# A third of the first token block's expert products moved to TensorE, and the softmax of the routing weights cut in two

## The chip, the cores and the metric

The kernel runs on one core of a Trainium2 chip. The metric is the device time of one execution in microseconds (us), taken as the median of several runs. The engines are TensorE (PE; its weight loads are shown as PEld), VectorE (DVE), ScalarE (ACT), GpSimd (POOL) and SyncE (SP). Each takes its own instructions in order and waits on semaphores for the others.

## The reference, cut to what matters

One block of a model: 256 tokens of 2048 values, a modulation, a mixer of two attention-like groups, and then a layer of 16384 single-neuron experts (PEER). Only the expert layer is touched. For each token, 8 heads choose 16 experts each:

```python
vs, pos = lax.top_k(cand, PEER_TOPK)          # 16 of the pairs of keys, for each token and head
idx = e1 * N_KEYS + e2                        # which expert
g = jax.nn.softmax(vs, axis=-1)               # routing weights over the 16
def block(args):                              # for a block of 128 tokens
    xb, ib, gb = args
    u = jnp.take(expert_down, ib, axis=0)     # 128 tokens x 8 heads x 16 rows of 2048 values
    a = jax.nn.gelu(jnp.einsum('td,thkd->thk', xb, u), approximate=False)
    w = (gb * a).astype(xb.dtype)
    vv = jnp.take(expert_up, ib, axis=0)
    return jnp.einsum('thk,thkd->td', w, vv)
```

## The kernel before, in words

The tokens lie on the 128 partitions in two blocks, t = 0 and t = 1. After the mixer, the hidden values `hf` (features on the partitions) are turned by TensorE into `ht[t]` (tokens on the partitions) by `by_tokens`. `head_scores(h)` computes a head's query and its scores against the keys, on TensorE. `head(t, h)` then finds the 16 chosen experts of a head for a block: `keys` (top 16 of each half, then of the candidate sums, in `vs` and `pos`) and `chosen` (the indices into `idx[t]`), all on DVE. It puts 16 rows on the list `ready`.

A "row" in what follows is one such item (t, k): 128 expert rows of 2048 float32, one for each token of the block, 1.05 MB in all. `issue` takes rows from `ready` and starts an indirect DMA from POOL for each (tile `rows`), as long as one of the buffers named in `homes` is free; a buffer tag has two buffers, so four tags make eight rows in flight. `dot` takes the oldest row in flight, and DVE multiplies it by `ht[t]` in place and adds it up into one column of `dots[t]`; then `issue` runs again, and the new DMA waits on POOL until that buffer has been read. There are 128 rows for a block, 256 in all. `ready` is kept sorted, so that all rows of t = 0 go ahead of those of t = 1.

The order of everything from here on is the program's order on each engine, kept by the wrapper `InOrder`. That wrapper is why nearly all these instructions carry line 69 in the profile; they are told apart by their tiles. The loop over `behind` runs the heads (0,1) to (0,7) and then (1,1) to (1,7), with `dot` between them: a head of t = 0 comes when at most two rows of t = 0 wait, one of t = 1 when at most eight rows of it wait and none of t = 0. After head (0,7) comes `softmax(0)`: DVE subtracts the largest score, ACT takes the exponential, DVE sums, inverts and scales, so that `ev[0][:, 2]` (tile `e`) holds the routing weights. `turned(0, [0, 1])` turns the expert numbers on TensorE. When the last row of t = 0 has been taken, `first_half` calls `turned(0, [2])` (ACT: Gelu of `dots[0]`; DVE: product with the weights; TensorE turns it) and emits `first_ones` and `gates` for the eight groups of 16 tokens of the first block. These build one-hot matrices on ACT (tiles `o`), multiply them on TensorE into a map of gate values, copy it out on ACT (`stage`, `kept`) and send it to device memory (`gd`). They run beside the rows of t = 1.

After head (1,7) the same is done for t = 1: `softmax(1)`, `turned(1, [0, 1])`, six `first_ones` on ACT, and the rows that are left. Then come `turned(1, [2])`, the gates of the second block, and a long last stage in which TensorE multiplies the gate map by the expert table `up` (a quarter of the columns is taken by gathered rows `upr` on DVE).

Of the kernel before, what the change touches and what calls it, by code (L numbers as in the profile page):

```python
# [7 lines left out]
F32 = mybir.dt.float32  # L8
# [4 lines left out]
AF = mybir.ActivationFunctionType  # L13
ALU = mybir.AluOpType
# [4 lines left out]
P = 128  # L19
D = 2048  # L20
KD = D // P
# [12 lines left out]
PEER_H = 8  # L34
# [46 lines left out]
def hybrid_block(ctx: ExitStack, tc: tile.TileContext, x, c, wada, cst, shp, wst, wg, wmv, wfv,  # L81
                 wmo, wout, wq, down, up, upr, out):
    nc = tc.nc
# [7 lines left out]
    def bank(shape, tag="ps"):  # L91
        return psum.tile(shape, F32, tag=tag, name=tag)
# [57 lines left out]
    ident = sh[:, 0:P]  # L150
# [79 lines left out]
    issue = [0]  # L230
# [109 lines left out]
    def gemm_p(src, rh, rl, w=None):  # L340

        wh, wl = w or weights(src, [P, KD, P])
        some_ada()
        o = bank([P, T])
        for k in range(KD):
            nc.tensor.matmul(o, wh[:, k], rh(k), start=(k == 0), stop=False)
            nc.tensor.matmul(o, wh[:, k], rl(k), start=False, stop=False)
            nc.tensor.matmul(o, wl[:, k], rh(k), start=False, stop=(k == KD - 1))
        return o
# [7 lines left out]
    def gemm_t(src, dst, ch):  # L357

        o = [bank([P, 512]) for _ in range(NT)]
        for kq in range(4):  # L360
# [9 lines left out]
            if kq == 3:  # L370
                for t in range(NT):
# [15 lines left out]
                                 op1=ALU.bypass)  # L387
# [208 lines left out]
    for b in range(KD):  # L596
        o = gemm_p(wout[b], lambda k: cath[k // 8][:, k % 8], lambda k: catl[k // 8][:, k % 8])
        g = mod[:, GATE1 * KD + b:GATE1 * KD + b + 1]
# [11 lines left out]
    hf = const.tile([P, KD, T], F32, tag="hs", name="hf")  # L610
# [36 lines left out]
    nc = AllInOrder(tc, nc)  # L647
# [12 lines left out]
    pg = ctx.enter_context(tc.tile_pool(name="pg", bufs=2))  # L660
    pk_cm = tc.tile_pool(name="pk", bufs=2)
    pk = pk_cm.__enter__()
# [64 lines left out]
    ev = [pb.tile([P, 3, PEER_H, TOPK], F32, name=f"e{t}", bufs=1) for t in range(NT)]  # L727
    idx = [pb.tile([P, HK], U32, name=f"idx{t}", bufs=1) for t in range(NT)]
    dots = [pg.tile([P, HK], F32, bufs=1, name=f"dots{t}") for t in range(NT)]

    def flat(tile, h0, h1):
        return tile[:, h0:h1].rearrange("p h k -> p (h k)")
# [31 lines left out]
    def issue():  # L764
        while ready:
            tag = homes[turn[0] % len(homes)]
            if sum(f[0] == tag for f in flight) == 2:
                return
            turn[0] += 1
            t, k = ready.pop(0)  # L770
            u = ring.tile([P, D], F32, tag=tag, name="rows", bufs=2)
            nc.gpsimd.indirect_dma_start(u, None, down, bass.IndirectOffsetOnAxis(ap=idx[t][:, k:k + 1], axis=0))
            flight.append((tag, t, k, u))

    def dot(n=1):

        for _ in range(n):
            if not flight:
                return
            _, t, k, u = flight.pop(0)  # L780
            nc.vector.scalar_tensor_tensor(u, u, 1.0, ht[t], op0=ALU.mult, op1=ALU.mult,
                                           accum_out=dots[t][:, k:k + 1])
            issue()

    def softmax(t):
        g = ev[t][:, 2]
        nc.vector.tensor_tensor(g, vs[t], vs[t][:, :, 0:1].to_broadcast([P, PEER_H, TOPK]), op=ALU.subtract)
        nc.scalar.activation(g, g, AF.Exp)
        gs = pk.tile([P, PEER_H], F32, tag="gs", name="gs")
        nc.vector.reduce_sum(gs, g, axis=AX.X)  # L790
        nc.vector.reciprocal(gs, gs)
        nc.vector.tensor_tensor(g, g, gs[:, :, None].to_broadcast([P, PEER_H, TOPK]), op=ALU.mult)

    def turned(t, parts):

        if 2 in parts:
            w = flat(ev[t][:, 2], 0, PEER_H)
            nc.scalar.activation(dots[t], dots[t], AF.Gelu)
            nc.vector.tensor_tensor(w, w, dots[t], op=ALU.mult)
        ep = bank([P, len(parts), P], "at")  # L800
        for i, p in enumerate(parts):
            nc.tensor.transpose(ep[:, i], flat(ev[t][:, p], 0, PEER_H), ident)
        nc.scalar.activation(est[t][:, parts[0]:parts[-1] + 1], ep, AF.Copy)
# [9 lines left out]
    def first_ones(tb, engine=None):  # L813

        half, t0 = divmod(tb * TB, P)
        if 2 * HB - 4 <= tb < 2 * HB - 2:
            o1 = px.tile([P, TB, P], F32, name="o1")
        else:
            o1 = (ring, pg)[tb % 2].tile([P, TB, P], F32, tag=("lo", "o1")[tb % 2], name="o1", bufs=2)
        if engine is None:  # L820
            for tl in range(TB):
                t = t0 + tl
                nc.scalar.activation(o1[:, tl], iota, AF.Abs, bias=est[half][:, 0, t:t + 1], scale=-1.0)
            nc.scalar.activation(o1, o1, AF.Relu, scale=-1.0, bias=one)
        else:
            engine.tensor_tensor(o1, iota[:, None, :].to_broadcast([P, TB, P]),
                                 est[half][:, 0, t0:t0 + TB, None].to_broadcast([P, TB, P]), op=ALU.is_equal)
        ones_at[tb] = o1

    def gates(tb):  # L830
        if not kept:
            kept.append(const.tile([P, GK, T, 8], F32, tag="hs", name="kept"))
        stage = pg.tile([P, 16 - GK, TB, 8], F32, tag=f"q{tb % 2 if tb >= HB else 0}", name="stage", bufs=1)
        ts = slice(tb * TB, (tb + 1) * TB)
        half, t0 = divmod(tb * TB, P)
        col = est[half]
        o1 = ones_at.pop(tb)
        for t8 in range(0, TB, 8):

            o2 = pg.tile([P, 8, P], F32, tag="o2", name="o2")  # L840
            for tl in range(8):
                t = t0 + t8 + tl
                if half:
                    nc.vector.tensor_scalar(o2[:, tl], iota, col[:, 1, t:t + 1], col[:, 2, t:t + 1],
                                            op0=ALU.is_equal, op1=ALU.mult)
                else:
                    nc.scalar.activation(o2[:, tl], iota, AF.Abs, bias=col[:, 1, t:t + 1], scale=-1.0)
            if not half:
                nc.scalar.activation(o2, o2, AF.Relu, scale=-1.0, bias=one)
                for tl in range(8):  # L850
                    t = t0 + t8 + tl
                    nc.scalar.activation(o2[:, tl], o2[:, tl], AF.Copy, scale=col[:, 2, t:t + 1])
                out_of_psum()
            for t4 in range(0, 8, 4):
                gp = bank([P, 4, P], "at")
                for i in range(4):
                    nc.tensor.matmul(gp[:, i], o1[:, t8 + t4 + i], o2[:, t4 + i], start=True, stop=True)
                full.append((gp, stage, tb, t8 + t4))
            if half:
                out_of_psum()  # L860
# [14 lines left out]
    def head_scores(h):  # L875
        qs = [query(2 * h)]
        qs.append(query(2 * h + 1))
        scores(2 * h, qs[0])
        if h == 0:
            for j in range(4):  # L880
                by_tokens(0, j)
        scores(2 * h + 1, qs[1])

    def head(t, h):
        keys(h, t, later[t][:, h])
        chosen(t, h, h + 1)
        issue()

    def waiting(t):
        return sum(r[0] == t for r in ready)  # L890
# [3 lines left out]
    def first_half():  # L894

        of_first = sum(f[1] == 0 for f in flight) + waiting(0)
        if halves[0] == 0 and of_first == 8:
            homes[:] = ["raw", "rawb", "hi"]
            halves[0] = 1
        if halves[0] == 1 and of_first == 0:  # L900
            halves[0] = 2
            turned(0, [2])
            for tb in range(4):
                first_ones(tb)
            for tb in range(HB):
                gates(tb)
                if tb + 4 < HB:
                    first_ones(tb + 4)
            out_of_psum()
# [11 lines left out]
    for i, (t, h) in enumerate(behind):  # L921
        while waiting(t) > (2, 8)[t] or (t and waiting(0)):
            dot()
            first_half()
        head(t, h)
        if i < 2:
            head_scores(4 + 2 * i)
            head_scores(5 + 2 * i)
        if i == 1:
            homes[:] = ["raw", "rawb", "hi", "lo"]  # L930
        if (t, h) == (0, PEER_H - 1):
            halves[0] = 0
            softmax(0)
            turned(0, [0, 1])
    softmax(1)
    turned(1, [0, 1])
    pk_cm.__exit__(None, None, None)
    px_cm = tc.tile_pool(name="px", bufs=2)
# [30 lines left out]
    while flight:  # L969
        dot()  # L970
        if len(ready) == 4:
            homes[:] = ["raw", "rawb"]
    turned(1, [2])
    steps = [(b, q) for b in range(P // 4) for q in range(KU // 4)]
    loaded = [load(up[b, q], [P, 4, 512]) for b, q in steps[:4]]
# [29 lines left out]
    o = [bank([P, 2, T], "ps" if i < 4 else "at") for i in range(KU // 2)]  # L1005
# [45 lines left out]
    for s, (b, q) in enumerate(steps):  # L1051
# [13 lines left out]
        if b % 3 == 0 and q == 0 and later_mods:  # L1065
            k = later_mods.pop(0)
# [4 lines left out]
        for i in range(4):  # L1071
            ob = o[2 * q + i // 2][:, i % 2]
            cols = slice(i * P, (i + 1) * P)
            for j in range(4):
# [5 lines left out]
                                 stop=(b == P // 4 - 1 and j == 3 and i % 2 == 1), **flags)  # L1080
# [93 lines left out]
```

## Time and profile before

| | |
|---|---|
| median of three runs | 1920.65 us (1917.27 to 1929.78) |
| the profiled execution's own time | 1930.43 us |
| its span, first to last instruction | 1928.7 us |
| DVE busy | 1678.6 us (87%) |
| PE busy | 1269.6 us (66%) |
| ACT busy | 813.8 us (42%) |
| POOL busy | 832.9 us (43%) |
| rows of t = 0 and t = 1, with their heads | about 545 to 1332 us of the span |

Times in rows are microseconds from the span's start, unless marked ns. "Granted clock" is TensorE's clock as a share of 2.4 GHz: 1.00 is the upper of its two levels, 0.50 the lower, 1.2 GHz. "DMA share" is the mean busy share of the core's 16 DMA engines; it can read a little over 1. A row in which an engine is said to wait names the last thing it waited for.

### The profile page before, as it was taken

The page shows a single profiled execution, that of the slowest core. Times are in us where ns is not written, and L with a number is a line of the kernel's source. Part 1 is how long each engine was busy: PE and PEld are TensorE (multiplying, and loading weights), DVE is VectorE, ACT ScalarE, POOL GpSimd, SP SyncE. Part 2 cuts the span into 40 slices and gives each one's busy share as a digit, 9 for nine tenths or more (in the row PEclk, how much of TensorE's full clock was granted, in tenths as well). Part 3 has the DMA queues.
Part 4 walks back from the last instruction along what each step waited for, and adds up shares of the span by engine and source line. Part 5 has one row for each costly group of instructions (what it writes and reads, how often), then busy time and mean ns, then how long its engine had stood idle before and what let it go on. Part 6 is the DMA issues. An engine that isn't in the chain of part 4 may idle for free. (4 is left out here: it accounts for less than half of the span.)

```text
span 1928.7 us, 24437 instructions
## 1 busy us (share of the span) xinstructions
PE 1269.6 (66%) x9078; PEld 1189.8 (62%) x9078; DVE 1678.6 (87%) x2383; ACT 813.8 (42%) x1324; POOL 832.9 (43%) x516
## 2 busy tenths in 40 slices
PE   5899999998999910000022111203699999999998
PEld 3899977798987810000022111103699999999998
DVE  7888898897788799999999999789788888988884
ACT  4332384585431000000195444491555555555552
POOL 0000000000003466776766677573267777677760
PEclk9999999999999965555556555556899999999999
DMA  9977767787869999999999999988699999999992
GB/s 395 370 314 291 283 257 302 289 326 282 326 252 398 421 376 405 378 385 365 422 369 394 389 366 382 363 322 338 229 368 349 352 377 378 374 369 391 369 349 100
DMA packets 126648, 663.70 MB, mean 344 GB/s; under 512 B 13377, under 2 KB 38337, under 8 KB 55745
## 3 DMA queue, kind: packets, MB, share of 16 engines
q1 hardware_dynamic: 69186, 326.58, 44.3%
q0 software_dynamic: 57344, 335.58, 43.4%
q8 instruction: 71, 1.16, 0.2%
q14 instruction: 47, 0.39, 0.0%
HBM read 647.42 MB, written 14.68 MB: 343 GB/s over the span
## 5 line engine op out<-in xcount | busy, mean ns | idle before, releaser
L69 POOL DMA_INDIRECT rows<-in_down,idx x256 | 477.6, 1866 | 843.2 <-DMA raw<-in_wq 579.6
L69 DVE SCALAR_TENSOR_TENSOR rows<-rows,ht 128x2048 f32<-128x2048 f32 x256 | 572.6, 2287 | 35.3 <-DMA rows<-in_down,idx 34.4
L69 POOL DMA_INDIRECT rows<-in_upr,idx x256 | 355.1, 1387 | 201.1 <-DVE acc L69 88.1
L69 PE MATMUL ps<-w,whi 128*128 128x256 f32 x2048 | 353.9, 278 | 9.3 <-ACT w L69 8.6
L69 PEld LDWEIGHTS ps<-w,whi 128*128 128x128 f32 x2048 | 310.8, 189 | 9.8 <-ACT w L69 8.8
L69 PE MATMUL ps<-w,wlo 128*128 128x256 f32 x1024 | 284.1, 277 | 0.0
L69 PE MATMUL at<-o,o 128*128 128x128 f32 x512 | 93.3, 361 | 249.4 <-ACT o L69 240.2
L69 PEld LDWEIGHTS at<-o,o 128*128 128x128 f32 x512 | 88.2, 266 | 254.6 <-ACT o L69 244.2
L69 PE MATMUL at<-sh,e 128*128 128x128 f32 x6 | 2.2, 433 | 347.3 <-DVE e L69 347.3
L69 PEld LDWEIGHTS at<-sh,e 128*128 128x128 f32 x6 | 1.1, 206 | 348.2 <-issue 348.2
L69 PEld LDWEIGHTS ps<-w,wlo 128*128 128x128 f32 x1024 | 193.4, 189 | 0.0
L69 DVE SCALAR_TENSOR_TENSOR acc<-rows,e,acc 128x512 f32<-128x512 f32 x254 | 189.2, 745 | 2.7 <-DMA rows<-in_upr,idx 1.1
L69 PE MATMUL at<-w,wht 128*128 128x256 f32 x1536 | 189.5, 283 | 0.0
L69 PEld LDWEIGHTS at<-w,wht 128*128 128x128 f32 x1536 | 186.4, 192 | 0.0
L69 ACT ACTIVATE whi<-raw 128x1024 fp32r<-128x1024 f32 x128 | 128.6, 1053 | 116.2 <-PE ps L69 67.8
L69 DVE TENSOR_TENSOR wlo<-raw,whi 128x1024 fp32r<-128x1024 f32 x128 | 155.5, 1218 | 23.7 <-ACT whi L69 22.1
L113 ACT ACTIVATE whi<-raw 128x2048 fp32r<-128x2048 f32 x65 | 124.1, 1911 | 117.3 <-PE at L315 24.9
L114 DVE TENSOR_TENSOR wlo<-raw,whi 128x2048 fp32r<-128x2048 f32 x65 | 148.4, 2285 | 24.5 <-ACT whi L113 24.3
L69 PE MATMUL ps<-hf,raw 128*128 128x256 f32 x512 | 116.4, 388 | 7.7 <-DMA raw<-in_wq 6.5
L69 ACT ACTIVATE wht<-raw 128x1024 fp32r<-128x1024 f32 x64 | 64.4, 1054 | 116.0 <-PE at L69 101.1
L69 PEld LDWEIGHTS ps<-hf,raw 128*128 128x128 f32 x512 | 98.4, 194 | 23.7 <-DMA raw<-in_wq 9.0
L69 ACT ACTIVATE o<-sh,est 128x128 f32<-128x128 f32 x352 | 105.9, 393 | 0.4 <-PE at L69 0.4
(248 smaller groups left out, 2750.3 us busy)
## 6 DMA issues: line engine op xcount, KB each, us to landing
raw<-in_up SPq DMA_DIRECT2D x96, 1024.0 KB
raw<-in_wada SPq DMA_DIRECT2D x45, 1024.0 KB
early<-in_wada SPq DMA_DIRECT2D x44, 1024.0 KB
raw<-in_wst SPq DMA_DIRECT2D x32, 1024.0 KB
raw<-in_wout SPq DMA_DIRECT2D x16, 1024.0 KB
raw<-in_wq SPq DMA_DIRECT2D x16, 1024.0 KB
gd<-stage SPq DMA_DIRECT2D x16, 768.0 KB
g<-gd SPq DMA_DIRECT2D x12, 1024.0 KB
```

Of the source, the lines that this page charges most:

```text
L69: return self.tc.keep_in_program_order(f(*args, **kwargs))
L113: nc.scalar.activation(hi, raw, AF.Copy)
L114: nc.vector.tensor_tensor(lo, raw, hi.bitcast(F32), op=ALU.subtract)
```

## The change: what it does

- From head (0,2) on (`by_pe[1]`), every third row of t = 0 by the running count goes to `pe_dot` in place of DVE's product. TensorE turns the row's sixteen 128x128 parts (four to a bank of tag "ps"), ACT copies each bank to a tile `ut` (tag "o1"), and `issue` starts the next gather, which waits on POOL until TensorE has read the row.
- `cross` multiplies the turned row by `hf` in 16 accumulating matmuls, so that a 128x128 product of all tokens' rows with all tokens' hidden values stands in a bank. It is emitted one `pe_dot` later, behind the next row's transposes.
- `diagonal` takes the diagonal of that product on DVE: one 128x128 multiplication by the identity with a sum, into the column of `dots[0]`. It is emitted two rows after `cross`. `all_crossed` does what is left when the last row of t = 0 has been taken, ahead of `turned(0, [2])`.
- `softmax(t)` is cut: `exps(t)` (subtraction and exponential) stays where `softmax(t)` was; the sum, inverse and scaling come later. For t = 0 that is directly ahead of `turned(0, [2])`, for t = 1 when four rows are left in `ready`. The small tile `gs` moves from pool `pk` to pool `pg`.

```diff
+    by_pe = [0, False]
+    turning = []
+    crossed = []
+
+    def pe_dot(k, u):
+        ut = pg.tile([P, KD, P], F32, tag="o1", name="ut")
+        for j in range(4):
+            tp = bank([P, 4, P], "ps")
+            for i in range(4):
+                nc.tensor.transpose(tp[:, i], u[:, (4 * j + i) * P:(4 * j + i + 1) * P], ident)
+            nc.scalar.activation(ut[:, 4 * j:4 * j + 4], tp, AF.Copy)
+        if crossed:
+            cross(*crossed.pop(0))
+        crossed.append((k, ut))
+
+    def cross(k, ut):
+        o = bank([P, P], "at")
+        for i in range(KD):
+            nc.tensor.matmul(o, ut[:, i], hf[:, i, 0:P], start=(i == 0), stop=(i == KD - 1))
+        turning.append((k, o, by_pe[0] + 2))
+
+    def diagonal(k, o):
+        d = pk.tile([P, P], F32, tag="tk", name="d")
+        nc.vector.scalar_tensor_tensor(d, o, 1.0, ident, op0=ALU.mult, op1=ALU.mult, accum_out=dots[0][:, k:k + 1])
+
+    def all_crossed():
+        while crossed:
+            cross(*crossed.pop(0))
+        while turning:
+            diagonal(*turning.pop(0)[:2])
+
     def dot(n=1):
         for _ in range(n):
             if not flight:
                 return
             _, t, k, u = flight.pop(0)
+            by_pe[0] += 1
+            if by_pe[1] and t == 0 and by_pe[0] % 3 == 0:
+                pe_dot(k, u)
+                issue()
+                continue
+            if turning and turning[0][2] <= by_pe[0]:
+                diagonal(*turning.pop(0)[:2])
             nc.vector.scalar_tensor_tensor(u, u, 1.0, ht[t], op0=ALU.mult, op1=ALU.mult,
                                            accum_out=dots[t][:, k:k + 1])
             issue()
 
-    def softmax(t):
+    def exps(t):
         g = ev[t][:, 2]
         nc.vector.tensor_tensor(g, vs[t], vs[t][:, :, 0:1].to_broadcast([P, PEER_H, TOPK]), op=ALU.subtract)
         nc.scalar.activation(g, g, AF.Exp)
-        gs = pk.tile([P, PEER_H], F32, tag="gs", name="gs")
+
+    def softmax(t):
+        g = ev[t][:, 2]
+        gs = pg.tile([P, PEER_H], F32, tag="gs", name="gs", bufs=1)
         nc.vector.reduce_sum(gs, g, axis=AX.X)
...
@@ first_half
             halves[0] = 2
+            all_crossed()
+            softmax(0)
             turned(0, [2])
...
@@ the loop over behind
         if i == 1:
             homes[:] = ["raw", "rawb", "hi", "lo"]
+            by_pe[1] = True
         if (t, h) == (0, PEER_H - 1):
             halves[0] = 0
-            softmax(0)
+            exps(0)
             turned(0, [0, 1])
-    softmax(1)
+    exps(1)
     turned(1, [0, 1])
...
         if len(ready) == 4:
             homes[:] = ["raw", "rawb"]
+            softmax(1)
     turned(1, [2])
```

## Rows read from the trace of the kernel before

**Rows 1.** The page: its span, the engines' busy time, the granted clock in 40 slices.

```profile
span 1928.7 us, 24437 instructions
PE 1269.6 (66%) x9078; PEld 1189.8 (62%) x9078; DVE 1678.6 (87%) x2383; ACT 813.8 (42%) x1324; POOL 832.9 (43%) x516
...
PEclk9999999999999965555556555556899999999999
```

**Rows 2.** Windows: stretch, length, engines' busy time (instructions), granted clock, DMA share, GB/s.

```profile
680.30:956.70 276.40, 4.73 (x24) 3.65 (x22) 271.06 (x384) 4.61 (x8) 194.54 (x102) 0.51 0.95 387
956.70:1243.40 286.70, 51.79 (x225) 48.10 (x225) 273.80 (x436) 153.13 (x434) 194.55 (x101) 0.57 0.96 385
1243.40:1332.30 88.90, 7.99 (x34) 7.30 (x34) 68.90 (x65) 57.08 (x148) 50.37 (x24) 0.50 0.85 341
```

**Rows 3.** Groups of 680.3 to 956.7: busy us, mean ns, idle before.

```profile
L69 DVE SCALAR_TENSOR_TENSOR rows<-rows,ht 128x2048 f32<-128x2048 f32 x104 | 231.0, 2284 | 1.4 <-DMA rows<-in_down,idx 0.9 <-issue 0.4
L69 POOL DMA_INDIRECT rows<-in_down,idx x102 | 194.8, 1910 | 88.9 <-DVE rows L69 59.7 <-issue 27.2 <-DVE tk L69 1.5
```

**Rows 4.** Timeline, DVE: start and end of head (0,3), first product behind it.

```profile
713.28 0.29 DVE L69 MAX8 kv<-later 128x8 f32<-128x128 f32 x1
...
721.75 0.17 DVE L69 SCALAR_TENSOR_TENSOR idx<-e 128x16 uint32<-128x16 f32 x1
721.84 2.28 DVE L69 SCALAR_TENSOR_TENSOR rows<-rows,ht 128x2048 f32<-128x2048 f32 x1
```

**Rows 5.** Windows of 8 us at and below the most that the DMA engines moved.

```profile
630.00:638.00 8.00, 7.91 (x41) 6.92 (x40) 6.60 (x7) 1.04 (x3) 5.41 (x5) 1.00 1.02 424
686.00:694.00 8.00, 0.00 (x0) 0.00 (x0) 8.00 (x9) 0.46 (x1) 7.08 (x4) 0.63 0.69 252
694.00:702.00 8.00, 0.00 (x0) 0.00 (x0) 7.29 (x7) 0.00 (x0) 6.78 (x5) 0.50 0.98 380
1224.00:1232.00 8.00, 0.00 (x0) 0.00 (x0) 6.90 (x7) 0.00 (x0) 7.09 (x4) 0.50 1.02 420
```

**Rows 6.** Timeline: sixteen transposes, their four copies, and 128-column float32 matmuls.

```profile
600.48 1.91 PE L69 MATMUL at<-sh,hf 128*128 128x128 f32 x16
601.23 2.08 ACT L69 ACTIVATE ht<-at 128x512 f32<-128x512 f32 x4
1245.66 3.79 PE L69 MATMUL at<-o,o 128*128 128x128 f32 x16 [31.52 <-ACT o L69]
1374.35 2.12 PE L69 MATMUL at<-o,o 128*128 128x128 f32 x16 [0.34 <-issue]
```

**Rows 7.** Windows around such matmuls: PE busy and granted clock.

```profile
1245.00:1250.00 5.00, 3.79 (x16) 3.49 (x16) 0.00 (x0) 4.97 (x18) 0.00 (x0) 0.50 0.31 119
1208.00:1216.00 8.00, 3.56 (x16) 3.37 (x16) 8.00 (x7) 4.52 (x13) 6.78 (x5) 0.79 1.01 376
1352.00:1356.00 4.00, 1.94 (x16) 1.75 (x15) 4.00 (x9) 1.01 (x4) 0.00 (x0) 1.00 0.70 191
1372.00:1376.00 4.00, 3.66 (x33) 3.50 (x32) 3.18 (x13) 0.69 (x3) 3.09 (x4) 1.00 0.98 301
```

**Rows 8.** Groups, DVE, 400 to 560: a product read from PSUM.

```profile
L600 DVE SCALAR_TENSOR_TENSOR xt<-ps,mod,xt 128x256 f32<-128x256 f32 x16 | 7.7, 480 | 10.6 <-PE ps L348 10.6
```

**Rows 9.** Timeline from `softmax(1)` to the last row: ACT and DVE.

```profile
1240.48 0.49 ACT L69 ACTIVATE stage<-at 128x384 f32<-128x384 f32 x1 [27.90 <-DMA gd<-stage]
...
1243.17 0.28 DVE L69 TENSOR_TENSOR e<-vs 128x128 f32<-128x128 f32 x1
...
1258.51 0.31 ACT L69 ACTIVATE e<-e 128x128 f32<-128x128 f32 x1
...
1258.85 0.29 DVE L69 TENSOR_REDUCE gs<-e 128x8 f32<-128x128 f32 x1 [15.39 <-ACT e L69]
...
1297.48 2.00 ACT L69 ACTIVATE o<-o,one 128x2048 f32<-128x2048 f32 x1
...
1329.29 2.29 DVE L69 SCALAR_TENSOR_TENSOR rows<-rows,ht 128x2048 f32<-128x2048 f32 x1 [1.42 <-DMA rows<-in_down,idx]
```

## The prediction, made before the change was run

> **What bounds the kernel now.** I read the page first, for the engines' shares and the clock by slices [rows 1], and then cut the time into the stretches in which the changed code runs, with the view of windows [rows 2]. The first runs from the end of head (0,2), where the change switches TensorE on, to the last row of t = 0; the second to the end of head (1,7); the third to the last row of t = 1. What the reader is to see: in the first stretch DVE is busy 271.1 of 276.4 us and TensorE 4.7; the DMA engines show a share of 0.95, so they have a little left, not much. The groups and their waits [rows 3] say the same from the other side: DVE waits for a row only 0.9 us in all, POOL waits 59.7 us for DVE to give back a buffer. So DVE ends last there. Its time is 104 products of 2.22 us (231.0 us) and five heads, each some 8.5 us from its first instruction to the next product [rows 4], 43 us; the two make 274.
>
> The next limit lies close behind. Where DVE does not hold it back, the DMA moves 420 to 424 GB/s at a share of 1.02 [rows 5]. A row of 1.05 MB then takes 2.48 us; the first stretch takes 276.4 / 104 = 2.66 us a row. All that DVE can be relieved of beyond this difference is lost to the DMA.
>
> **Part one, the products on TensorE.** From the 25th row of t = 0 to the 128th, those whose number can be divided by three are 34 rows (27, 30, ..., 126). DVE loses 34 x 2.22 = 75.5 us and gains 34 diagonals. No row of the trace has one; the nearest is a product of twice the width from PSUM, 0.48 us [rows 8], and below it lies nothing, so 0 to 16 us; I take the upper end, since reading out the sum adds a little. DVE then needs about 217 us for the 104 rows, 2.1 a row, and no longer ends last.
>
> The DMA does. In the first stretch it moved 387 GB/s x 276.4 us = 107 MB; at 422 GB/s that takes 253.5 us, 22.9 less. That is the upper end. Not all of it comes: after head (0,2), taken with six buffers, the DMA engines have run dry (252, then 380 GB/s in two windows of 8 us [rows 5]), which costs (170 + 42) / 422 x 8 = 4 us, and this precedes any help by TensorE. At the end of t = 0 DVE now waits for the last `cross` and its diagonal, then runs the scaling of `softmax(0)` (some 0.8 us), moved from behind head (0,7); I put 2 us on the wait and the rest together. That leaves 17; I take 16. The lower end, nothing, is the second rival below.
>
> TensorE's own price: sixteen transposes in 1.91 us, 1024 columns' worth of float32 matmuls (8 of them, two records each) in 2.12 us, both at the upper clock [rows 6, 7]. A row is 16 transposes and 16 matmuls: 1.9 + 4.2 = 6.1 us. Three rows of DMA take 7.45 us. So at 2.4 GHz TensorE is busy some 80% and keeps up, with an idle gap of about 1.3 us in each round. At the lower clock the eight matmuls took 3.79 us [rows 6, 7], the transposes I estimate at twice 1.91, and a row takes 3.8 + 7.6 = 11.4 us, more than three rows take today (276.4 / 34 = 8.1 us). The clock decides the part. It is 0.50 when the stretch begins. But while TensorE is behind it has no gap at all, and after bursts as short as those of the first block's gates (3.6 busy in 8 us) the granted clock already averages 0.79; with 1.9 us busy in 4, inside the second block's gates, it holds 1.00 [rows 7]. I take the upper clock for nearly all rows, and cover the cold start with the slack: eight buffers hold 20 us of DMA.
>
> Here a rule speaks against the change. The trace shows sixteen transposes in 1.91 us at a granted clock that is full in that stretch [rows 1, 6], but in the midst of long matmuls, so it can't say what transposes alone would be granted. The Trainium skill ("TensorE: Matmul & The Clock Gate", Part 4: PE-mode transpose) says that transposes don't count as TensorE being busy in the same way, and don't bring the full clock. By that rule a third of TensorE's time here would not hold the clock up, and the sum could be the first rival's, 2018 us, in place of 1890; no row of this kernel settles it.
>
> What lies beside other work: ACT's four copies a row cost 2.08 us [rows 6], 34 x 2.08 = 71 us in a stretch where ACT is busy 4.6 [rows 2]; nothing waits behind them but the exponential of `exps(0)`, which nobody needs soon. Without that cover they would be 71 us. The gather that follows a TensorE row waits on POOL until its transposes are done; later gathers queue behind it. At the upper clock that is about 2 us after landing, no later than a DVE product ends, and six other rows are in flight. `diagonal` waits on DVE for `cross`; behind it stands the next product, two rows after the TensorE row. With transposes and `cross` done 6.1 us after that row landed, and two more rows landed at 5.0, DVE waits about 1 us in every 7.45, time which it has. During a head DVE takes no row for 8.5 us; some six rows are still to land, 15 us of DMA, so the DMA is covered.
>
> **Part two, the softmax cut in two.** At `softmax(0)` the round trip over ACT cost DVE 0.4 us, nothing to speak of. At `softmax(1)` it costs 15.39 us [rows 9]: ACT has been held up by `gd` (27.9 us), has two groups of gates and their copies ahead of the exponential, and DVE, with rows landed, stands. The third stretch moves only 341 GB/s [rows 2]. After the change DVE goes on with products; the sum and the scaling come some 12 rows before the end, 25 us and more after the exponential. Its 30 products need 30 x 2.22 = 67 us. The stretch's bytes, 341 x 88.9 = 30.3 MB, need 72 us at 422 GB/s: so at most 17 us come back. ACT's six `first_ones` end 41 us after the exponential, at 1299.5, and the last product at 1331.6 [rows 9]; 15 us earlier would still be 1316, so ACT does not become late. I take 15, with 8 to 17 for the range.
>
> **The sum.** 16 + 15 = 31 us. Behind the last row all work (gates of the second block, the last stage on TensorE) only moves forward. The profiled execution took 1930.4 us (span 1928.7), 10 above the median; 31 us off it makes 1899. Off the median, 1920.65 - 31 = 1890 us.
>
> **The rivals.** First, on the other side: TensorE stays at 1.2 GHz. For it speaks that its work is broken by waits in each round, and that no row shows what clock transposes of landing rows would be granted; the gates of the first block, with bursts of 3.6 us, fall back to 0.50 [rows 7]. Against it, the busy share of 80% and the gaps of little over 1 us. At 11.4 us a row 34 rows take 388 us where the stretch takes 276, 112 us more, less the 15 of the softmax: +97, 2018 us. It decides from the point where a TensorE row takes 8.1 us on average (the first part loses) or 8.6 (the whole change loses), which is a mean granted clock of about 0.7.
>
> Second, the first part yields nothing: TensorE is behind about as much as DVE was before (a mean of 8.1 us a row, by gaps and copies), or POOL, in order, holds back gathers behind TensorE rows so that the DMA stays at 387 GB/s. Only the softmax counts: 1906 us.
>
> Third, the second part yields nothing, since the third stretch is near the DMA's limit once the rows flow again, or ACT becomes late for `softmax(1)`: 1905 us. Fourth, neither part yields anything, 1921 us: DVE's relief is taken up by waits on `cross`, and the stall reappears at `softmax(1)`.
>
> **How the numbers follow.** The forecast of 1890 has 0.62, TensorE at the lower clock 0.12, only the softmax 0.16, only the products 0.06, neither 0.04. Within 1% of 1920.65 is 1901 to 1940, about what a measurement of this kernel can tell from no change. Faster by over 1%: the forecast and a little of the single-part cases, 0.64; slower by over 1%: 0.13; within: 0.23. The forecast's own range is 23 + 17 = 40 at most, with 6 us of scatter in the median more, so 1874, and 14 less than forecast on the other side. The upper end takes in the two cases in which one part alone counts, with the same scatter: 1912. That holds 0.84 by the chances above.
>
> **What would show it.** In the changed profile the first stretch should be about 16 us shorter, at over 410 GB/s, with DVE waiting for rows and 34 diagonals of about 0.4 us; TensorE should be granted nearly 1.00 and show some 6 us for each row. DVE's wait of 15.4 us for the exponential should be gone, and the third stretch be 72 to 75 us long. If the granted clock in the first stretch lies under 0.7, or POOL waits on TensorE, part one has failed. If DVE waits at `softmax(1)` or ACT's `first_ones` end after the last row, part two has.

## The result, and the profile after

The changed kernel took 1899.6 us, median of four runs (1893.8 to 1906.0), beside 1924.1 for the kernel before (1917.3 to 1929.8): a ratio of 0.9873, with a 95% interval from 0.9845 to 0.9901. That is 24.5 us less; 31 were forecast, and 1890 us. The 1890 were reckoned from 1920.65 us; beside the changed kernel the kernel before took 1924.1, so 3.5 of the 9.6 us between forecast and result lie in the base. The profiled execution took 1906.0 us, its span is 1904.3. Two executions in the experiments below, one of the kernel before (2243.6 us) and one with every second row on TensorE (4165.7 us), stand far outside all others and are in no ratio.

The page of the changed kernel, beside [rows 1]: TensorE is busy 203 us more, DVE 65 less, and the lower clock now begins only where the rows of t = 0 end.

```profile
span 1904.3 us, 27885 instructions
PE 1472.5 (77%) x10710; PEld 1387.7 (73%) x10710; DVE 1613.5 (85%) x2383; ACT 886.2 (47%) x1460; POOL 834.6 (44%) x516
...
PEclk9999999999999999999955555556899999999999
```

The three stretches of [rows 2] in the changed kernel's windows, and the two windows of 8 us behind head (0,2) that answer to [rows 5]. The columns are as there.

```profile
685.20:950.90 265.70, 204.14 (x1646) 198.42 (x1644) 206.19 (x385) 76.77 (x144) 188.93 (x104) 0.94 0.99 406
950.90:1236.10 285.20, 56.00 (x241) 51.59 (x241) 273.29 (x435) 159.78 (x454) 194.81 (x98) 0.53 0.96 384
1236.10:1310.60 74.50, 4.22 (x18) 3.69 (x18) 68.95 (x65) 50.18 (x128) 52.87 (x24) 0.52 1.00 403
685.00:693.00 8.00, 5.55 (x44) 5.04 (x43) 7.96 (x9) 3.95 (x9) 2.75 (x1) 1.00 0.47 197
693.00:701.00 8.00, 3.90 (x35) 3.71 (x33) 4.25 (x7) 1.12 (x3) 6.69 (x5) 0.96 0.93 353
```

The reader is to see the first stretch at 265.7 us in place of 276.4 and at 406 GB/s in place of 387, with DVE busy 206 us only; the second the same (285.2 and 286.7); the third at 74.5 in place of 88.9. The windows of the third stretch are not cut at quite the same instructions. From DVE's subtraction (1243.17 us before, [rows 9], and 1236.13 after, shown below) to its product of the weights with the last Gelu, in the kernel before

```profile
1331.96 0.29 DVE L69 TENSOR_TENSOR e<-e,dots 128x128 f32<-128x128 f32 x1 [0.38 <-ACT dots L69]
```

and in the changed kernel

```profile
1310.92 0.29 DVE L69 TENSOR_TENSOR e<-e,dots 128x128 f32<-128x128 f32 x1 [0.38 <-ACT dots L69]
```

it took 88.8 us and now takes 74.8. In what follows "the last product" is this one. From the end of head (0,2) to it the changed kernel is 25.9 us shorter (625.8 in place of 651.7). What lies behind it took 593.4 us (1904.3 - 1310.9) in place of 596.7, and the part ahead of head (0,2), which the change does not touch, ended at 685.2 in place of 680.3; the next section shows that this 4.9 is scatter.

Where the gain of the first stretch lies, windows of 16 us behind the heads (0,4) to (0,7) show. While DVE works on a head, it gives back no buffer. In the kernel before, the DMA runs short each time:

```profile
765.00:781.00 16.00, 0.00 (x0) 0.00 (x0) 15.96 (x15) 0.00 (x0) 11.25 (x6) 0.50 0.86 331
813.00:829.00 16.00, 0.00 (x0) 0.00 (x0) 16.00 (x15) 0.00 (x0) 13.87 (x8) 0.50 0.83 312
853.00:869.00 16.00, 0.00 (x0) 0.00 (x0) 15.96 (x17) 0.00 (x0) 11.60 (x6) 0.50 0.86 327
901.00:917.00 16.00, 0.00 (x0) 0.00 (x0) 16.00 (x15) 0.00 (x0) 13.40 (x7) 0.50 0.77 276
```

In the changed kernel, behind the same heads, it nearly keeps its rate:

```profile
765.00:781.00 16.00, 13.23 (x103) 12.91 (x102) 14.01 (x19) 5.01 (x11) 11.54 (x6) 0.89 1.02 421
809.00:825.00 16.00, 13.82 (x107) 13.50 (x108) 13.54 (x19) 4.90 (x9) 12.94 (x8) 0.89 1.01 401
853.00:869.00 16.00, 11.02 (x96) 10.70 (x96) 14.98 (x21) 4.13 (x8) 14.02 (x7) 1.00 1.00 396
891.00:907.00 16.00, 15.58 (x136) 15.23 (x134) 14.33 (x21) 5.79 (x11) 14.02 (x6) 0.98 1.02 412
```

Measured against 422 GB/s, the four windows before lose 17 us and those of the changed kernel 2.

Who waited for whom in the first stretch, the waits that bear on the rows (us, times, longest). Before, DVE waited 0.9 us for rows there [rows 3]; now it waits 30, and TensorE 55. POOL waits only 4.6 us for TensorE, so the gathers are not held back behind its rows, as one form of the second rival had it.

```profile
PE ps L69 <- DMA rows<-in_down,idx: 55.3, 30, 6.4
POOL rows L69 <- DVE d L69: 30.4, 12, 8.5
DVE rows L69 <- DMA rows<-in_down,idx: 30.1, 19, 3.2
DVE d L69 <- PE at L69: 25.8, 20, 2.7
POOL rows L69 <- DVE rows L69: 22.1, 3, 11.9
...
POOL rows L69 <- PE ps L69: 4.6, 12, 1.2
```

One round of three rows from the changed kernel's timeline: sixteen transposes as a row lands, the matmuls of the row before it, ACT's copies, a product, the diagonal with its wait of 0.81 us, a product.

```profile
786.61 1.94 PE L69 MATMUL ps<-sh,rows 128*128 128x128 f32 x16 [1.95 <-DMA rows<-in_down,idx]
787.33 2.06 ACT L69 ACTIVATE ut<-ps 128x512 f32<-128x512 f32 x4 [5.39 <-PE ps L69]
...
788.38 3.74 PE L69 MATMUL at<-hf,ut 128*128 128x128 f32 x32
789.05 2.29 DVE L69 SCALAR_TENSOR_TENSOR rows<-rows,ht 128x2048 f32<-128x2048 f32 x1 [1.83 <-DMA rows<-in_down,idx]
...
792.16 0.29 DVE L69 SCALAR_TENSOR_TENSOR d<-at,sh 128x128 f32<-128x128 f32 x1 [0.81 <-PE at L69]
792.37 2.29 DVE L69 SCALAR_TENSOR_TENSOR rows<-rows,ht 128x2048 f32<-128x2048 f32 x1
...
794.05 1.94 PE L69 MATMUL ps<-sh,rows 128*128 128x128 f32 x16 [1.93 <-DMA rows<-in_down,idx]
```

From one first transpose to the next are 7.44 us, three rows of DMA; TensorE works 5.7 of them. At the end of head (1,7), in the same timeline, DVE goes on 0.2 us after its subtraction, 10 us ahead of the exponential, where it had stood for 15.39 [rows 9]:

```profile
1236.13 0.28 DVE L69 TENSOR_TENSOR e<-vs 128x128 f32<-128x128 f32 x1
1236.33 2.28 DVE L69 SCALAR_TENSOR_TENSOR rows<-rows,ht 128x2048 f32<-128x2048 f32 x1
...
1246.39 0.31 ACT L69 ACTIVATE e<-e 128x128 f32<-128x128 f32 x1
...
1284.70 0.28 DVE L69 TENSOR_REDUCE gs<-e 128x8 f32<-128x128 f32 x1
```

### The profile page after: what moved, and what is told of

It reads as the page before. It is cut to its first block, busy times and chain, and to the rows that moved or that the text cites. A ratio compares the mean times of both kernels' runs of the same rounds, so it can differ in the third digit from the quotient of the medians.

```text
span 1904.3 us, 27885 instructions
## 1 busy us (share of the span) xinstructions
PE 1472.5 (77%) x10710; PEld 1387.7 (73%) x10710; DVE 1613.5 (85%) x2383; ACT 886.2 (47%) x1460; POOL 834.6 (44%) x516
## 5 line engine op out<-in xcount | busy, mean ns | idle before, releaser
L69 DVE SCALAR_TENSOR_TENSOR rows<-rows,ht 128x2048 f32<-128x2048 f32 x222 | 500.7, 2287 | 65.9 <-DMA rows<-in_down,idx 65.5
L69 DVE TENSOR_TENSOR wlo<-raw,whi 128x1024 fp32r<-128x1024 f32 x128 | 155.4, 1218 | 27.6 <-ACT whi L69 27.3
L69 ACT ACTIVATE ut<-ps 128x512 f32<-128x512 f32 x136 | 72.3, 602 | 174.5 <-PE ps L69 174.4
L69 PE MATMUL at<-hf,ut 128*128 128x128 f32 x1088 | 132.4, 282 | 0.0
L69 PEld LDWEIGHTS at<-hf,ut 128*128 128x128 f32 x1088 | 130.4, 200 | 0.0
L69 PE MATMUL ps<-sh,rows 128*128 128x128 f32 x544 | 75.4, 298 | 55.4 <-DMA rows<-in_down,idx 55.3
```

Source lines behind the costliest of these rows:

```text
L69: return self.tc.keep_in_program_order(f(*args, **kwargs))
```

## The experiments

**The changed kernel and the kernel before once more.** No edit.

> The changed kernel once more, in five rounds, for a narrower interval and a second profile. By the stretches of the two profiles the change gives 11 to 12 us between head (0,2) and the last row of t = 0, 1 between there and head (1,7), 14 from there to the last product and 3 behind it, some 30 us in all; the stretch ahead of head (0,2), which the change does not touch, was 4.9 us longer in the changed kernel's profile. If that is scatter, five rounds give 1.2 to 1.6% (23 to 31 us). If something of the change costs time there, they give the 1.2% again and the second profile shows the 5 us again.

> The kernel before once more, one look, to see how much the stretch ahead of head (0,2) scatters from one profiled execution to the next. If the 4.9 us are scatter, head (0,2) ends here some us away from 680.4; if they belong to the change, within 1 us of it.

Measured: 0.988 of the kernel before (0.9859 to 0.9901), 25.7 us less by the medians. Head (0,2) ended at 680.9 us in this profile of the changed kernel and at 676.5 in this one of the kernel before, against 685.2 and 680.3 in the first two. So the stretch ahead of the change scatters by some 4 us in either kernel. In this pair the changed kernel is again the later one; but among the profiles of whole kernels the eight with rows on TensorE lie between 676.4 and 685.2 and the three without between 676.5 and 680.3, so nothing shows that the 4.9 us belong to the change. The three stretches were 264.4, 286.5 and 75.4 us long, within 1.5 us of the first profile.

The second profile of the kernel before held a surprise: 610.2 us behind its last product (1938.9 - 1328.7), where the first had 596.7. The chain that ended last, in order of time (start, length, what), shows it in the last stage. Here is a piece of it from the first profile of the kernel before:

```profile
1472.31 10.88 PE ps L69 x96
1483.19 5.76 PE at L69 x48
```

and a piece from the second, of the same program:

```profile
1591.21 11.31 PE ps L69 x96
1602.52 5.76 PE at L69 x48
```

TensorE waits for nothing in either piece, at a granted clock of 1.00; three steps of 144 matmuls take 16.64 us in the one and 17.07 in the other, and 32 such rounds make 13.8 us.

**Each part alone.** In the first kernel the softmax is whole again, at its old places; in the second no row goes to TensorE.

```diff
             all_crossed()
-            softmax(0)
...
             exps(0)
+            softmax(0)
...
     exps(1)
+    softmax(1)
...
-            softmax(1)
```

> Every third row on TensorE, the softmax in one piece at its old places. Theory (two parts that add, the first limited by DMA): 8 to 14 us faster than before, with DVE's wait of some 15 us for the exponential of t = 1 back in place. Rival (the rows on TensorE bring nothing by themselves, the stall at the softmax was the whole gain): within 4 us of before.

```diff
-            by_pe[1] = True
```

> The softmax cut in two, all rows on DVE. Theory: 13 to 17 us faster than before, the first stretch at its 276 us and 387 GB/s, no wait for the exponential. Rival (the stretch behind head (1,7) is held by the DMA, so the stall only moves): under 6 us. Rival (the stall was the whole gain): 23 us or more.

Measured: with the rows alone 0.9922 (0.9892 to 0.9952), some 15 us (13.7 by the medians), where 8 to 14 were expected. DVE's wait for the exponential is back, though shorter than before (15.39 us [rows 9]):

```profile
1240.22 0.28 DVE L69 TENSOR_REDUCE gs<-e 128x8 f32<-128x128 f32 x1 [10.08 <-ACT e L69]
```

With the softmax alone it was 0.9981 (0.9966 to 0.9995), some 3.7 us, where 13 to 17 were expected. This was a miss on the whole kernel. Its profile, however, has the subtraction at 1243.7 us and the last product at 1319.5, 75.8 us in place of 88.8 and 88.5 in the two profiles of the kernel before: the stretch is as short as in the changed kernel. Its last stage ran at the slowest spacing of all:

```profile
1856.21 11.52 PE ps L69 x96
1867.73 5.60 PE at L69 x48
```

That is 17.12 us a round, and 611 us behind the last product. The gain was there in the stretch and was not in the time. Whether it was lost to this spacing or by the change itself is the question of the last group of runs.

**More and fewer rows on TensorE.**

```diff
-            if by_pe[1] and t == 0 and by_pe[0] % 3 == 0:
+            if by_pe[1] and t == 0 and by_pe[0] % 2 == 0:
```

> Every second row of t = 0 on TensorE in place of every third. Theory (the gathers are the limit at 2.48 us a row, and TensorE needs 5.65 us for one of its rows at the upper clock): two rows of DMA take 4.97 us, less than TensorE's 5.65, so TensorE ends last: 52 x 5.65 = 294 us for the stretch to the last row of t = 0, some 29 us longer than with every third, POOL waiting for TensorE, granted clock 1.00; the whole about as fast as before or 5 us slower. Rival (DVE's relief is what counts): the stretch gets shorter or stays at 265 us.

The same line with 5 in place of 3:

> Every fifth row of t = 0 on TensorE, 21 rows in place of 34. Theory (the gathers are the limit): DVE then needs 83 x 2.22 + 21 x 0.3 + 43 = 234 us of the stretch, still under the 258 of the DMA, so the stretch stays within 4 us of 265 and the whole within 5 us of the changed kernel; TensorE has 5.65 us of work in 12.4, and where its clock falls a row takes 11.3, still within. Rival (DVE's relief is what counts): the stretch is 13 x 1.9 = 25 us longer times the third that TensorE took, 7 to 10 us longer.

With every second row the time was 0.9995 (0.9973 to 1.0016) of the kernel before, and the stretch to the last row of t = 0 was 283.8 us long (681.5 to 965.3), 18 more than with every third. TensorE ended last, as the window of that stretch and its groups show (the idle time before each group and what ended it stand behind the bar):

```profile
685.00:965.00 280.00, 277.81 (x2502) 277.11 (x2500) 166.83 (x380) 111.63 (x215) 135.00 (x104) 1.00 0.96 392
```

```profile
L69 POOL DMA_INDIRECT rows<-in_down,idx x104 | 135.0, 1298 | 146.7 <-PE ps L69 66.0 <-DVE d L69 31.1 <-DVE rows L69 26.1
L69 DVE SCALAR_TENSOR_TENSOR rows<-rows,ht 128x2048 f32<-128x2048 f32 x51 | 116.6, 2287 | 8.9 <-DMA rows<-in_down,idx 5.2 <-issue 3.6
```

TensorE is busy 277.8 of 280 us, POOL waits 66 us for it, DVE is down to 167 us and nothing is gained by that. The 294 us expected were 10 too many: back to back a row costs 277.8 / 52 = 5.3 us, not 5.65. With every fifth row the stretch was 266.1 us (679.9 to 946.0) and the time 0.9878 (0.9849 to 0.9906), the same as with every third, though TensorE took 21 rows in place of 34 and its granted clock was 0.77:

```profile
685.00:946.00 261.00, 151.63 (x1005) 148.30 (x1003) 224.92 (x378) 52.66 (x90) 180.30 (x102) 0.77 1.00 406
```

DVE has 19 us more to do (225 us in place of 206), the DMA moves the same 406 GB/s, and the stretch is as long. So the DMA holds it, not DVE's work.

**Transposes alone.** The matmuls of `cross` are replaced by transposes; these rows' products are left out.

```diff
-        o = bank([P, P], "at")
-        for i in range(KD):
-            nc.tensor.matmul(o, ut[:, i], hf[:, i, 0:P], start=(i == 0), stop=(i == KD - 1))
-        turning.append((k, o, by_pe[0] + 2))
+        o = bank([P, 4, P], "at")
+        for i in range(2 * KD):
+            nc.tensor.transpose(o[:, i % 4], ut[:, i // 2], ident)
+        turning.append((k, o[:, 0], by_pe[0] + 2))
```

> The 16 matmuls of each row on TensorE are replaced by 32 more transposes, so that TensorE does nothing but transposes for about the same time in a round (16 x 0.12 + 32 x 0.12 = 5.7 us); the products of these rows are left out and the output is not the reference's. Theory (transposes hold the clock up like any other work): granted clock 0.9 or more in the stretch, 265 us. Rival (transposes don't bring the full clock): granted clock near 0.50, 11.4 us a row, the stretch 380 us or more.

One execution took 1902.9 us. In the window of the stretch TensorE, with nothing but transposes (1629 recorded, and two of expert numbers), is granted 0.94, as with the products:

```profile
685.00:944.00 259.00, 197.65 (x1631) 190.91 (x1629) 201.84 (x380) 75.78 (x143) 187.24 (x104) 0.94 1.00 410
```

**Heads moved to where DVE has time.** DVE is now idle for 60 of the 266 us of the first stretch, and busy for 273 of 285 in the second, seven heads among it. Four of these are moved ahead.

```diff
-    behind = [(t, h) for t in range(NT) for h in range(1, PEER_H)]
+    behind = [(0, 1), (0, 2), (0, 3), (1, 1), (0, 4), (1, 2), (0, 5), (1, 3), (0, 6), (1, 4), (0, 7), (1, 5), (1, 6), (1, 7)]
...
-        while waiting(t) > (2, 8)[t] or (t and waiting(0)):
+        early = t == 1 and h < 5
+        while waiting(0) > 10 if early else waiting(t) > (2, 8)[t] or (t and waiting(0)):
```

> Four heads of t = 1 are moved between the heads of t = 0, where DVE now waits for rows. Theory (in the first stretch the DMA is the limit and DVE has 55 us to spare, in the second DVE is the limit): the first stretch stays within 5 us of 265, the second falls from 285 to 260 or 265, where the DMA's 422 GB/s hold it, and the whole is 15 to 25 us faster than the changed kernel, 1.9 to 2.5% faster than before. Rival (DVE is still the limit in the first stretch, through its waits on the cross products): the four heads, 34 us, come on top of the first stretch and nothing is won. Rival (the gates of the first block on ACT end last): the rows end earlier, but the wait for the exponential comes back before the last rows.

Measured: 0.9989 (0.9971 to 1.0007), all of the gain gone, by the last of the rivals. Its first two stretches were 273 and 265 us long, 538 together where the changed kernel's took 551:

```profile
677.50:950.50 273.00, 206.98 (x1649) 201.18 (x1648) 236.31 (x521) 77.36 (x144) 173.41 (x104) 0.92 0.98 396
950.50:1215.50 265.00, 45.38 (x193) 41.77 (x193) 245.96 (x299) 136.10 (x381) 208.82 (x98) 0.51 1.00 409
```

So head (1,7) did end some 13 us earlier, counted from head (0,2). But the timelines of ACT and DVE show the exponential at 1282, the wait at the second half of the softmax back, and the last Gelu at 1325, behind ACT's six `first_ones`:

```profile
1278.78 0.49 ACT L69 ACTIVATE stage<-at 128x384 f32<-128x384 f32 x1 [15.80 <-DMA gd<-stage]
...
1282.41 0.31 ACT L69 ACTIVATE e<-e 128x128 f32<-128x128 f32 x1
...
1282.75 0.29 DVE L69 TENSOR_REDUCE gs<-e 128x8 f32<-128x128 f32 x1 [18.46 <-ACT e L69]
...
1325.02 0.29 DVE L69 TENSOR_TENSOR e<-e,dots 128x128 f32<-128x128 f32 x1 [18.95 <-ACT dots L69]
```

From the end of head (0,2) to the last product are 647.6 us, 21 to 22 more than in the two profiles of the changed kernel, about what the whole kernel lost. ACT's waits say why; in the changed kernel's second profile (from 945 to the last product) they are 125.8 us in six waits for the transfers of `gd`, in this one 161.7 in seven:

```profile
ACT stage L69 <- DMA gd<-stage: 161.7, 7, 27.4
```

There is one buffer `stage` for the first block's gates, so each group waits for the transfer of the one before it. That these transfers take longer because the gathers now move 409 GB/s beside them, in place of 384, is likely but was not shown. So a second buffer was given to it, in the place of `ht0`, which nobody reads any more by then:

```diff
-        stage = pg.tile([P, 16 - GK, TB, 8], F32, tag=f"q{tb % 2 if tb >= HB else 0}", name="stage", bufs=1)
+        stage = pg.tile([P, 16 - GK, TB, 8], F32, tag=f"q{tb % 2}" if tb >= HB else ("q0", "ht0")[tb % 2], name="stage", bufs=1)
```

> Four heads of t = 1 moved ahead as before, and a second buffer for the stage tile of the first block's gates (in the place of ht0, which nobody reads once the rows of t = 0 are done), so that ACT does not wait each time for the previous transfer to device memory. Theory (with the heads moved, ACT's gates and those waits ended last): the wait of ACT for that transfer falls from 162 us to under 60, the exponential comes before the last 12 rows, the last product ends at about 1290 us, and the whole is 12 to 20 us faster than the changed kernel, 1.9 to 2.3% faster than before. Rival (the transfers themselves are held up by the gathers, so that two buffers only fill): the exponential still comes after 1260, and nothing is won.

Measured: 0.9832 (0.9809 to 0.9854), 1891.1 us beside 1924.0. ACT's wait for `gd` fell to 40.8 us, the exponential came at 1214.3, at once behind the subtraction, and the last product at 1286.6. That is 610.2 us behind the end of head (0,2), 16 less than in the two profiles of the changed kernel (625.8 and 626.4):

```profile
ACT e L69 <- DVE e L69: 55.9, 1, 55.9
ACT stage L69 <- DMA gd<-stage: 40.8, 5, 14.4
```

By its ratio this version beats the changed kernel too, by 0.4% or 0.5% (0.9832 beside 0.9873 and 0.988); its interval stands clear of the second's and overlaps a little with the first's, and the two kernels were not run side by side. That is 8 to 9 us, less than the 12 to 20 expected, and the last stage went over to the round of 17.07 us half-way through in the profiled execution. How much of the shortfall this is was not measured.

**The last stage cut off.** To take the spacing of the last stage out, three kernels keep 12 of its 96 steps and none of its gathered rows: the kernel before, the softmax alone, and the whole change. All three also clear the tile `mod` at the start, and the ends of the last stage's loops are set to fit.

```diff
+    nc.vector.memset(mod, 0.0)
...
-    left = [(t, k) for t in range(NT) for k in range(HK)]
+    left = []
...
-    steps = [(b, q) for b in range(P // 4) for q in range(KU // 4)]
+    steps = [(b, q) for b in range(4) for q in range(KU // 4)]
```

> The kernel before with its last stage cut to 12 of 96 steps and without the gathered rows of that stage (the output is not the reference's); the measure for the next two. In the whole kernels the last stage's matmuls came at one of three steady spacings (16.64, 17.07 or 17.12 us for a round of three steps) whatever the kernel, which makes up to 15 us between executions. If that is where most of the scatter comes from, these runs lie within 6 us of each other, around 1430 to 1470 us.

> The same cut with only the softmax parted. Theory (the 12 us that the profile shows between head (1,7) and the last product are real and come through to the stages behind; the 3.7 us measured on the whole kernel are the spacing of the last stage on top): 10 to 14 us less than the cut kernel before. Rival (the gain is given back behind the last product, or ahead of the stretch): 1 to 6 us less, as on the whole kernel.

> The same cut of the changed kernel. Theory (two parts that add): 22 to 28 us less than the cut kernel before, that is 11 to 14 less than the cut kernel with the softmax alone. Rival (the softmax gives nothing that lasts): 12 to 18 us less than the cut kernel before.

| cut kernel | median us (lowest to highest of 4) | less than before |
|---|---|---|
| before | 1456.8 (1453.4 to 1457.6) | |
| softmax alone | 1444.4 (1441.5 to 1452.2) | 12.5 |
| whole change | 1429.6 (1425.7 to 1431.3) | 27.3 |

The softmax's 12.5 us are real, and the rows on TensorE bring 14.8 more; no run of one cut kernel reaches into the times of another. In the profile of the cut kernel before, the stall that the softmax's cut takes away was

```profile
1253.73 0.29 DVE L69 TENSOR_REDUCE gs<-e 128x8 f32<-128x128 f32 x1 [10.55 <-ACT e L69]
```

The runs of one cut kernel lie within 4 to 11 us of each other, where 6 were expected, the 17 runs of the whole kernel before in the first group of experiments within 12. So the spacing of the last stage is not the only source of scatter.

## Why the prediction was right, point by point

*What bounds.* DVE ended last in the first stretch and the DMA stood close behind: the moved rows gained 10.7 to 12 us of that stretch's 276 and not the 65 us that DVE lost there in busy time (271 to 206). With DVE's part raised again (every fifth row), nothing changed. What was gained are in the main the DMA's dips behind the heads, 17 us before and 2 after.

*Part one* was put at 16 us: 14.8 in the cut kernels, 15 alone on the whole kernel, 11 and 12 by the stretches of two profiles (276.4 to 265.7 and 264.4). The DMA's limit of 422 GB/s held for most windows, but the average was 406: the dip behind head (0,2) was deeper than before (197 and 353 GB/s in place of 252 and 380 [rows 5]) and cost (225 + 69) / 422 x 8 = 5.6 us where 4 were allowed. Some later windows ran at 388 to 403. The diagonal took 0.29 us and 0.08 to read out its sum, under the upper end of [rows 8]; DVE waited for `cross` 0.8 us a round, where 1 was forecast, in time that it had.

*TensorE's price* was put at 6.1 us a row and was 5.7 (1.94 + 3.74), at a granted clock of 0.94. The first rival, the lower clock, did not come about. The page of the Trainium skill ("TensorE: Matmul & The Clock Gate", Part 4: PE-mode transpose), by which transposes would not bring the full clock, does not agree with these runs: with transposes alone the clock was the same 0.94 over 259 us. That TensorE ends last when its rows cost more than the DMA's was shown from the other side, by every second row.

*Part two* was put at 15 us: 12.5 in the cut kernels, 13 to 14 by the profiles' third stretch. The term was taken from one profile's stall of 15.39 us, and the stall is not that long in every execution: 10.55 in the cut kernel before, 10.08 with the rows alone. It is gone and nothing took its place; the floor of 72 us that the bytes set was almost reached (74.5 and 75.4).

*The sum* was 31 and measured 24.5 and 25.7 on the whole kernel, 27.3 without the last stage. No step failed; by the cut kernels the two terms were 1 and 2.5 us too large, and the rest of the difference lies within the scatter of the whole kernel. The second and the third rival, in which one part brings nothing, are refuted by the cut kernels. On the whole kernel the softmax alone seemed to come close to the third (3.7 us), and its profile shows a slow last stage. If that stage's spacing was the slow one in more of its 12 runs than in those of the kernel before, it would explain the difference; but only profiled executions show the spacing, and the kernel before's own profile in that group had a slow one too (17.07), so it stays open.

## What to carry to other kernels

Before moving work off the busiest engine, work out what the next limit leaves: here DVE was relieved of 65 us and the DMA let 11 to 15 of them through, and a third or a fifth of the rows gave the same. Then look where the relieved engine has become idle, and move its other work there, but follow the chain of every engine that runs beside it: ACT, for which DVE waits only 0.4 us in the changed kernel's last two stretches, took the whole gain back until its one transfer buffer was doubled. A stall read from one profile is one sample; read a second one before it becomes a term. And where a change is worth 1%, measure it on the kernel cut down to the stage in question.

## What the runs showed of the hardware that was not expected

- The long stretch of matmuls in the last stage settled into one of several steady spacings, at a granted clock of 1.00 and without a wait: 16.64, 17.07 or 17.12 us for 144 matmuls. One and the same program, the kernel before, had 16.64 in one profile and 17.07 in another. Of eleven profiles of whole kernels six had 16.64, three 17.07 or 17.12, and two went from 16.64 to 17.07 half-way. It is worth 14 us of 1900, over half of what was to be measured.
- Transposes of 128x128 float32 held the upper clock as well as the mix with matmuls did: a granted clock of 0.94 over 259 us with transposes alone, and 0.94 over the changed kernel's first stretch.
